# A float32 decoder trunk with routed experts on one core: the order of ScalarE and VectorE instructions around the small expert groups

## The chip, the cores and the metric

The kernel runs on one NeuronCore of one Trainium2 chip. The metric is the device time of one execution in microseconds (us); lower is better. A core has a matrix engine (TensorE, PE in the profile, with its weight loads as PEld), VectorE (DVE), ScalarE (ACT), GpSimd (POOL) and SyncE (SP), which here issues nearly all DMA transfers. Each engine works through its own queue of instructions in the order in which the program holds them, and waits at an instruction until the semaphores that it needs are set.

## The reference, cut to what matters

Two layers; the first has a dense SwiGLU, the second a mixture of eight experts of which each token takes two. All is float32, with 256 tokens of width 1024 and 3584 hidden columns for each expert.

```python
def swiglu(h, wg, wu, wd):
    return (jax.nn.silu(h @ wg) * (h @ wu)) @ wd

def moe_swiglu(h, router, wg, wu, wd):
    ...
    out = jnp.zeros_like(h)
    for e in range(N_EXPERTS):
        out = out + gate_e[..., e:e + 1] * swiglu(h, wg[e], wu[e], wd[e])
    return out
```

## The kernel before

The expert layer takes most of the time: it begins at about 480 us of the profiled span and ends near 1386 us. The experts are sorted by how many tokens they have, and expert slots get 32, 64, 64 or 128 places (`SLOTS`). An expert with 128 places is worked on by class `Ffn` ("full"), one with 64 or 32 by class `Few` ("small"). The 3584 hidden columns are cut into 7 groups of 512. One step of the layer is one group of one expert, and `in_turn()` writes the order of the 56 steps out: 35 full ones and 21 small ones. Stretches in which full and small steps alternate stand at the beginning (small expert 1, 64 places), in the middle (small expert 3, 32 places, often two full steps to a small one) and at the end (small expert 7, 64 places); expert 5 has a stretch of full steps to itself.

A step has a gate product, an up product and, one step later, a transposition of their result (`turn`) and a down product (`down`). Each product reads 4 half tiles of weights of 128 x 1024 floats. For step `(e, g)` after `last` the loop does, in this order: `ffn[e].gate(g)`, `ffn[last[0]].turn(last[1])`, `ffn[e].up(g)`, `ffn[last[0]].down(last[1])`. So where a small step follows a full one, PE does the small gate product, transposes the full step's activations, does the small up product and then the down product of the full step.

A full step multiplies in three passes of a rounded format (`mm3`): every half tile is first split (`split`, lines 281 to 292) by ACT into a rounded part `whi` (L290) and by DVE into the rest `wlo` (L291). The pool `wsp` holds four of each, so a split can be made only when PE is done with the half tile four before. The activations are split likewise after the transposition, into `aTh` on ACT (L627) and `aTl` on DVE (L628). For each half of a down half tile `mm3` needs `whi` and `aTh` first, then `wlo`, then `aTl`. A small step needs no split: it multiplies the float32 tiles as they are (L675 for gate and up, L702 for down). Its activation is L681 on ACT, its product of gate and up L684 on DVE, and the copy of its transposed activations L692 on ACT. In a full step these are L607 and L616.

`Stream` brings the weights in the order in which they are used: its loads go into a ring of 14 tiles of 1 MB (`raw`, some of them in `hT`), and SP issues a load as soon as the ring's next tile is free. `more()` has up to `LEAD = 4` split half tiles traced ahead; tiles of small steps don't count. So during a full step's up product the program text has already split its four down half tiles, before the text of the small step's gate product comes to its end.

The text does not settle the order of an engine's queue. The framework's scheduler orders each queue by its own estimate of when an instruction can start, within the data dependences. `tc.issue_after(ins)` adds an edge: what is traced inside it stands behind `ins` in the queue of `ins`'s engine. The kernel has such an edge already for the transpositions, which stand behind the last matmul of the gate product of the next step (`ffn[e].mark`).

Of the kernel before, what the change touches and what calls it, by code (L numbers as in the profile page):

```python
# [10 lines left out]
F32 = mybir.dt.float32  # L11
# [3 lines left out]
AF = mybir.ActivationFunctionType  # L15
ALU = mybir.AluOpType
# [3 lines left out]
P = 128  # L20
# [76 lines left out]
def trunk(ctx: ExitStack, tc: tile.TileContext, a: dict, out: bass.AP):  # L97
    nc = tc.nc
    V, A, G, T = nc.vector, nc.scalar, nc.gpsimd, nc.tensor
# [160 lines left out]


    ring = [wraw] * RAW
    free, behind = [0], []
    turn = [0]

    def more_raw():
# [14 lines left out]
    def split(raw, shape, q):  # L281
        hi = wsp.tile([P, 1024], F32R, name="whi")
        lo = wsp.tile([P, 1024], F32R, name="wlo")
        half = raw[:, 1024 * q : 1024 * q + 1024]
        with ExitStack() as es:
            free[0] -= 1
            if free[0] < 0:
                for ins in behind:
                    es.enter_context(tc.issue_after(ins))
            A.activation(hi, half, AF.Copy)  # L290
            V.tensor_tensor(lo, half, hi.bitcast(F32), op=ALU.subtract)  # L291
        return [x.rearrange("p (a b) -> p a b", a=shape[0] // 2) for x in (hi, lo)]

    def by_quarter(src, shape):
# [8 lines left out]
    def weight(src, shape):  # L303
        raw = load(src, shape)
        return [split(raw, shape, q) for q in range(2)]
# [53 lines left out]
    with tc.tile_pool(name="rope0", bufs=1) as rp:  # L359
# [8 lines left out]
        for bits in (8, 9, 9):  # L368
            e = math.floor(math.log2(rest)) + 1 - bits
# [207 lines left out]
    class Ffn:  # L577
# [23 lines left out]
        def gate(self, g):  # L601
            def done(t, ps):
                s = self.s[g, t] = self.sp.tile([P, GW], F32, name="silu", bufs=2 * self.nt)
                if self.rs is None:
                    A.activation(s, ps, AF.Silu)
                else:
                    A.activation(s, ps, AF.Silu, scale=self.rs(t))  # L607
            self.product(self.wg, g, done)

        def up(self, g):  # L610
            def done(t, ps):
                s = self.s[g, t]
                if self.rs is None:
                    V.tensor_tensor(s, s, ps, op=ALU.mult)
                else:
                    V.scalar_tensor_tensor(s, ps, self.rs(t), s, op0=ALU.mult, op1=ALU.mult)  # L616
            self.product(self.wu, g, done)

        def turn(self, g):
            for t in range(self.nt):  # L620
                s = self.s.pop((g, t))
                pt = ptr.tile([P, 4, P], F32, name="ps_t")
                for c in range(4):
                    T.transpose(pt[:, c], s[:, c * P : (c + 1) * P], ident)  # L624
                hi = self.sp.tile([P, 4, P], F32R, name="aTh", bufs=self.nt)
                lo = self.sp.tile([P, 4, P], F32R, name="aTl", bufs=self.nt)
                A.activation(hi, pt, AF.Copy)  # L627
                V.tensor_tensor(lo, pt, hi.bitcast(F32), op=ALU.subtract)  # L628
                self.aT[g, t] = (hi, lo)

        def down(self, g, done):
# [23 lines left out]
    class Few:  # L655
# [22 lines left out]

        def gate(self, g):
            s = self.s[g] = self.sp.tile([P, self.nj * P], F32, name="silu", bufs=2)  # L680
            A.activation(s, self.product(), AF.Silu, scale=self.rs)  # L681

        def up(self, g):
            V.scalar_tensor_tensor(self.s[g], self.product(), self.rs, self.s[g], op0=ALU.mult, op1=ALU.mult)  # L684

        def turn(self, g):
            s = self.s.pop(g)
# [49 lines left out]
    def moe(i, norm, make_next):  # L737
# [74 lines left out]
        with ExitStack() as es:  # L812
            sp = es.enter_context(tc.tile_pool(name=f"mo{i}", bufs=1, reuse_waits="tile"))
            py = es.enter_context(tc.tile_pool(name=f"my{i}", bufs=1, space=PSUM, reuse_waits="tile"))
            xe, oh, ffn, place, of = {}, {}, {}, {}, {}
# [3 lines left out]
            def width(e):  # L819
                return SLOTS[RANKS[e]]  # L820

            def arrange():
# [27 lines left out]
                for src, dst in ((posm, posp), (gate, tokp[:, :, :NE])):  # L850
                    V.tensor_tensor(w, m[:, None].to_broadcast([P, NT, NE, NE]),
                                    src[:, :, None, :].to_broadcast([P, NT, NE, NE]), op=ALU.mult)
                    V.tensor_reduce(dst, w, axis=AX.X, op=ALU.add)
                V.tensor_copy(tokp[:, :, NE : NE + 1], tok[:, :, NE : NE + 1])

            def seat(e):

                oh[e] = [rt.tile([P, P], F32R, name=f"oh{t}") for t in range(NT)]
                for t in range(NT):
                    at = posp[:, t, e : e + 1]  # L860
                    w = width(e)
                    if w < P:
                        V.tensor_scalar(oh[e][t].rearrange("p (b n) -> p b n", n=w),
                                        row[:, None, :w].to_broadcast([P, P // w, w]), at, None, op0=ALU.is_equal)
                    else:
                        V.tensor_scalar(oh[e][t], row, at, None, op0=ALU.is_equal)
# [36 lines left out]
            def places(e):  # L903

                pb = ptr.tile([P, NT, P], F32, name="ps_t")
                for t in range(NT):
                    T.matmul(pb[:, t], (posp if e else posm)[:, t, e : e + 1].to_broadcast([P, P]), ident, start=True, stop=True)
                oT = sp.tile([P, NT, P], F32R, name="oT", bufs=2)
                c = C_COL + WIDTHS.index(width(e))
                V.tensor_scalar(oT, pb, cst[:, c : c + 1], None, op0=ALU.is_equal)  # L910
                place[e] = oT
# [3 lines left out]
            def weigh(e, n2):  # L915
                gs, ps = of[e][:, e : e + 1], ys[e][n2]
                yh = sp.tile([P, 512], F32R, name="yh")
                yl = sp.tile([P, 512], F32R, name="yl")
                A.activation(yh, ps, AF.Copy, scale=gs)
                V.scalar_tensor_tensor(yl, ps, gs, yh.bitcast(F32), op0=ALU.mult, op1=ALU.subtract)  # L920
                ys[e][n2] = (yh, yl)

            def scatter(e, n2, fed=None):
                (yh, yl), oT = ys[e][n2], place[e]
                cs = slice(512 * n2, 512 * n2 + 512)
                for t in range(NT):
                    pz = ptr.tile([P, 512], F32, name="ps_t")
                    T.matmul(pz, oT[:, t], yh, start=True, stop=False)
                    T.matmul(pz, oT[:, t], yl, start=False, stop=True)  # L929
                    V.tensor_tensor(xs[t][:, cs], xs[t][:, cs], pz, op=ALU.add)  # L930
                    if fed is not None:
                        fed.feed(t, n2)
# [33 lines left out]
            def enter(e):  # L966
                gather(e)
                slots(e)
# [3 lines left out]
            for n, (e, g) in enumerate(steps):  # L972
                over = [x for x in ends if ends[x] + 2 == n]
                if g == 0:
                    rs = of[e][:, NE : NE + 1]
                    if width(e) < P:
                        ffn[e] = Few(lambda k, x=xe[e]: x[:, k], rs, sp, py, stream, width(e), e % 2)
                    else:
                        ffn[e] = Ffn(None, None, None, lambda part, k, t, x=xe[e]: x[:, k, part], 1,
                                     lambda t, rs=rs: rs, sp, py, stream, e % 2)  # L980
                ffn[e].gate(g)
                for x in over:
                    scatter(x, 0)
                    weigh(x, 1)
                if last:
                    with tc.issue_after(ffn[e].mark):
                        ffn[last[0]].turn(last[1])
                ffn[e].up(g)
                if n == 0:
                    arrange()  # L990
                    seat(1)
                if n == 1 or g == NG - 1:
                    if coming < NE:
                        enter(coming)
                        coming += 1
                        if coming < NE:
                            seat(coming)
                    elif e % 2 == 0:
                        fin_g = hpool.tile([P, D], F32, name="mT0")
                        G.dma_start(fin_g, a["final_norm"].partition_broadcast(P))  # L1000
                for x in over:
                    scatter(x, 1)
                if last:
                    ffn[last[0]].down(last[1], lambda t, ps, e=last[0]: ys.update({e: list(ps)}))
                    if last[1] == NG - 1:
                        weigh(last[0], 0)
                if g == NG - 2:
                    places(e)
                last = (e, g)
# [4 lines left out]
            e = NE - 1  # L1014
# [180 lines left out]
```

## Time and profile before

| | |
|---|---|
| runs | 1395.58 us median of 3 (1394.84 to 1399.27) |
| profiled execution | 1398.9 us, of it 1397.0 us span of instructions |
| granted TensorE clock, mean | 0.988 |
| PE busy | 1351.0 us, 97% of the span |
| DVE, ACT busy | 925.4 us (66%), 783.8 us (56%) |
| HBM read | 426.80 MB |

The time is that of the whole execution; the span is what the engines' instructions cover in it. Busy shares are means over stretches with different limits, so each stretch has to be looked at by itself. A line "A <- B: t, n, m" of the waits says that A waited for B t us in all, n times, at most m us. In a timeline the text in brackets is the idle time of the engine before the instruction and what ended it. Matmuls overlap, and their ends are modelled, so the time from start to start is what counts.

### The profile page before, as it was taken

Reading aid. Unit: us, or ns where it says so; the run is one execution under the profiler, and the core shown is the slowest. Engines: PE = TensorE matmul, PEld = TensorE weight load, DVE = VectorE, ACT = ScalarE, POOL = GpSimd, SP = SyncE. Lnnn points to the kernel's source line nnn. Section 1 sums busy time; section 2 is a strip of 40 time slices with the busy share of each in tenths; the row PEclk is TensorE's granted clock in tenths of the full one; section 3 lists DMA queues with packets and bytes.
Section 4 is the critical chain, followed back from the end, with each engine's and each line's share of the span. In section 5 each row is a group of like instructions: output and inputs, shape, how many; then the busy total and the mean of one; then the engine's idle time right before and its main releaser. Section 6 shows DMA issues by size and latency. Waiting matters only on the chain. (4 is left out here: it accounts for less than half of the span.)

```text
span 1397.0 us, 20471 instructions
## 1 busy us (share of the span) xinstructions
PE 1351.0 (97%) x7737; PEld 1039.8 (74%) x7737; DVE 925.4 (66%) x1450; ACT 783.8 (56%) x1118; POOL 7.3 (1%) x17
## 2 busy tenths in 40 slices
PE   7999999999999999999999999999999999999995
PEld 6888888888798787777666777777777788766662
DVE  7887544444787876655545776785679888644553
ACT  6867444444677556544444665665567777444442
POOL 1000000000000000000000000000000000000000
PEclk9999999999999989999999999999999999999998
DMA  8334554555333788999999999999999998999970
GB/s 336 106 136 144 190 184 184 187 185 188 137 135 138 281 313 310 401 421 420 394 408 344 418 419 403 417 420 420 420 421 411 365 361 316 375 401 416 419 312 32
DMA packets 60680, 429.23 MB, mean 307 GB/s; under 512 B 7089, under 2 KB 7281, under 8 KB 8993
## 3 DMA queue, kind: packets, MB, share of 16 engines
q1 hardware_dynamic: 59920, 425.85, 77.0%
q0 software_dynamic: 656, 2.02, 0.4%
q8 instruction: 62, 1.02, 0.3%
q14 instruction: 42, 0.34, 0.1%
HBM read 426.80 MB, written 1.05 MB: 306 GB/s over the span
## 5 line engine op out<-in xcount | busy, mean ns | idle before, releaser
L291 DVE TENSOR_TENSOR wlo<-raw,whi 128x1024 fp32r<-128x1024 f32 x528 | 626.5, 1221 | 164.6 <-ACT whi L290 158.6
L290 ACT ACTIVATE whi<-raw 128x1024 fp32r<-128x1024 f32 x528 | 546.3, 1060 | 237.0 <-PE ps_y L339 117.4
L337 PE MATMUL ps_m<-whi,mT 128*128 128x512 f32 x624 | 251.7, 403 | 0.0
L338 PE MATMUL ps_m<-wlo,mT 128*128 128x512 f32 x624 | 250.1, 401 | 0.1
L339 PE MATMUL ps_m<-whi,mT 128*128 128x512 f32 x624 | 247.7, 397 | 0.0
L338 PE MATMUL ps_y<-wlo,aTh 128*128 128x512 f32 x392 | 158.2, 404 | 15.5 <-DVE wlo L291 15.5
L337 PE MATMUL ps_m<-whi,hT 128*128 128x512 f32 (+1 forms) x416 | 156.0, 376 | 0.5 <-ACT whi L290 0.4
L338 PE MATMUL ps_m<-wlo,hT 128*128 128x512 f32 (+1 forms) x416 | 155.3, 373 | 0.5 <-DVE wlo L291 0.5
L339 PE MATMUL ps_y<-whi,aTl 128*128 128x512 f32 x392 | 155.5, 397 | 0.0
L339 PE MATMUL ps_m<-whi,hT 128*128 128x512 f32 (+1 forms) x416 | 154.8, 372 | 0.0
L337 PE MATMUL ps_y<-whi,aTh 128*128 128x512 f32 x392 | 143.6, 405 | 0.8 <-ACT aTh L627 0.8
L338 PEld LDWEIGHTS ps_m<-wlo,mT 128*128 128x128 f32 x624 | 117.7, 189 | 32.3 <-DVE wlo L291 7.2
L337 PEld LDWEIGHTS ps_m<-whi,mT 128*128 128x128 f32 x624 | 117.7, 189 | 30.9 <-ACT whi L290 3.4
L339 PEld LDWEIGHTS ps_m<-whi,mT 128*128 128x128 f32 x624 | 117.8, 189 | 26.5
L675 PE MATMUL ps_m<-raw,mT 128*64 128x256 f32 (+1 forms) x1648 | 120.4, 327 | 0.0
L675 PEld LDWEIGHTS ps_m<-raw,mT 128*64 128x64 f32 (+1 forms) x1648 | 79.0, 123 | 39.4 <-issue 12.4
L628 DVE TENSOR_TENSOR aTl<-ps_t,aTh 128x512 fp32r<-128x512 f32 x49 | 33.1, 688 | 110.4 <-ACT aTh L627 110.4
L338 PEld LDWEIGHTS ps_y<-wlo,aTh 128*128 128x128 f32 x392 | 74.5, 190 | 39.3 <-DVE wlo L291 22.3
L681 ACT ACTIVATE silu<-ps_m,of 128x256 f32<-128x256 f32 (+1 forms) x21 | 9.2, 439 | 162.0 <-PE ps_m L675 162.0
L337 PEld LDWEIGHTS ps_y<-whi,aTh 128*128 128x128 f32 x392 | 73.3, 190 | 24.0 <-ACT whi L290 4.3
L337 PEld LDWEIGHTS ps_m<-whi,hT 128*128 128x128 f32 x416 | 78.5, 189 | 14.1 <-ACT whi L290 0.8
L338 PEld LDWEIGHTS ps_m<-wlo,hT 128*128 128x128 f32 x416 | 78.5, 189 | 13.8 <-DVE wlo L291 1.0
(215 smaller groups left out, 1281.7 us busy)
## 6 DMA issues: line engine op xcount, KB each, us to landing
raw<-in_moe_w_gate SPq DMA_DIRECT2D x104, 1024.0 KB, 9.1
raw<-in_moe_w_up SPq DMA_DIRECT2D x104, 1024.0 KB, 9.9
raw<-in_moe_w_down SPq DMA_DIRECT2D x103, 1024.0 KB, 9.7
raw<-in_w_in SPq DMA_DIRECT2D x18, 1024.0 KB, 6.9
raw<-in_dense_w_gate SPq DMA_DIRECT2D x14, 1024.0 KB, 4.8
raw<-in_dense_w_up SPq DMA_DIRECT2D x14, 1024.0 KB, 4.9
raw<-in_dense_w_down SPq DMA_DIRECT2D x14, 1024.0 KB, 4.8
raw<-in_w_out SPq DMA_DIRECT2D x8, 1024.0 KB, 4.8
```

What stands on the lines that cost most here:

```text
L290: A.activation(hi, half, AF.Copy)
L291: V.tensor_tensor(lo, half, hi.bitcast(F32), op=ALU.subtract)
L337: T.matmul(ps, xh, wh, start=start, stop=False)
L338: T.matmul(ps, xh, wl, start=False, stop=False)
L339: return T.matmul(ps, xl, wh, start=False, stop=stop).ins
L628: V.tensor_tensor(lo, pt, hi.bitcast(F32), op=ALU.subtract)
L675: self.mark = T.matmul(o, self.xT(k), wk[:, b], start=k == 0, stop=k == DK - 1).ins
L681: A.activation(s, self.product(), AF.Silu, scale=self.rs)
```

## The change

Four edges are added. `split` keeps its two instructions in `at_split`, and the copy of the transposed activations keeps its DVE instruction in `turned`. The small step's activation (gate) then stands on ACT behind the `whi` that was traced last; the `turn` of the step before it (transpositions, `aTh`, `aTl`) stands behind the last `whi` on ACT and the last `wlo` on DVE, where the present step is a small one; and the small step's product (up) stands on DVE behind the last `aTl`. No instruction is added or removed.

```diff
-    free, behind = [0], []
+    free, behind, at_split, turned = [0], [], [], []
...
-            A.activation(hi, half, AF.Copy)
-            V.tensor_tensor(lo, half, hi.bitcast(F32), op=ALU.subtract)
+            at_split[:] = [A.activation(hi, half, AF.Copy).ins, V.tensor_tensor(lo, half, hi.bitcast(F32), op=ALU.subtract).ins]
...
-                V.tensor_tensor(lo, pt, hi.bitcast(F32), op=ALU.subtract)
+                turned[:] = [V.tensor_tensor(lo, pt, hi.bitcast(F32), op=ALU.subtract).ins]
...
-            A.activation(s, self.product(), AF.Silu, scale=self.rs)
+            ps = self.product()
+            with tc.issue_after(at_split[0]):
+                A.activation(s, ps, AF.Silu, scale=self.rs)
...
-            V.scalar_tensor_tensor(self.s[g], self.product(), self.rs, self.s[g], op0=ALU.mult, op1=ALU.mult)
+            ps = self.product()
+            with ExitStack() as after:
+                if turned:
+                    after.enter_context(tc.issue_after(turned[0]))
+                V.scalar_tensor_tensor(self.s[g], ps, self.rs, self.s[g], op0=ALU.mult, op1=ALU.mult)
...
-                    with tc.issue_after(ffn[e].mark):
+                    with tc.issue_after(ffn[e].mark), ExitStack() as after:
+                        if width(e) < P:
+                            for ins in at_split:
+                                after.enter_context(tc.issue_after(ins))
                         ffn[last[0]].turn(last[1])
```

What the edges do to the queues shows in the program's rows (line, operation, output<-inputs, shape, how many in a row). First ACT in the last alternating stretch, one full and one small step, from the full step's gate activation on. Before:

```order
L607 ACTIVATE silu<-ps_m,of 128x512
L692 ACTIVATE aTh<-ps_t 128x256
L290 ACTIVATE whi<-raw 128x1024 x2
L681 ACTIVATE silu<-ps_m,of 128x256
L627 ACTIVATE aTh<-ps_t 128x512
L290 ACTIVATE whi<-raw 128x1024 x10
```

With the change (line numbers are those of the changed file: 606 for 607, 697 for 692, 682 for 681, 626 for 627):

```order
L606 ACTIVATE silu<-ps_m,of 128x512
L697 ACTIVATE aTh<-ps_t 128x256
L290 ACTIVATE whi<-raw 128x1024 x4
L682 ACTIVATE silu<-ps_m,of 128x256
L626 ACTIVATE aTh<-ps_t 128x512
L290 ACTIVATE whi<-raw 128x1024 x8
```

The two splits ahead of the small activation were the last two of the full step's up product; now the up product's four stand ahead of the full gate activation, the four of the down product ahead of the small activation and of `aTh`, and eight (next gate, next up) behind them.

DVE at the same place, from the full step's product of gate and up to the next one. Before:

```order
L616 SCALAR_TENSOR_TENSOR silu<-ps_m,of,silu 128x512
L628 TENSOR_TENSOR aTl<-ps_t,aTh 128x512
L684 SCALAR_TENSOR_TENSOR silu<-ps_m,of,silu 128x256
L291 TENSOR_TENSOR wlo<-raw,whi 128x1024 x12
```

With the change (615 for 616, 627 for 628, 689 for 684, 290 for 291):

```order
L615 SCALAR_TENSOR_TENSOR silu<-ps_m,of,silu 128x512
L290 TENSOR_TENSOR wlo<-raw,whi 128x1024 x4
L627 TENSOR_TENSOR aTl<-ps_t,aTh 128x512
L689 SCALAR_TENSOR_TENSOR silu<-ps_m,of,silu 128x256
L290 TENSOR_TENSOR wlo<-raw,whi 128x1024 x8
```

The four `wlo` of the down product stood behind `aTl` and behind the small step's product; now they stand ahead of both. In the first alternating stretch, before about 640 us, the queues of the two kernels are the same. SP's and POOL's queues are the same throughout.

## Rows read from the trace of the kernel before

**Rows 1.** The page, part 1: busy time of each engine.

```profile
PE 1351.0 (97%) x7737; PEld 1039.8 (74%) x7737; DVE 925.4 (66%) x1450; ACT 783.8 (56%) x1118; POOL 7.3 (1%) x17
```

**Rows 2.** Waits of PE, whole span: total us, times, longest.

```profile
PE ps_y L338 <- DVE wlo L291: 15.5, 15, 1.4
...
PE ps_t L899 <- DVE mT L893: 0.9, 1, 0.9
```

**Rows 3.** Waits of PE, 640 to 760 us.

```profile
PE ps_y L338 <- DVE wlo L291: 3.5, 3, 1.4
```

**Rows 4.** Waits of PE, 760 to 1000 us.

```profile
PE ps_y L338 <- DVE wlo L291: 5.7, 6, 1.0
```

**Rows 5.** Waits of PE, 1200 to 1360 us.

```profile
PE ps_y L338 <- DVE wlo L291: 6.3, 6, 1.1
```

**Rows 6.** Timeline of PE, one small step of 64 places: start, us, instruction.

```profile
1229.63 3.67 PE L675 MATMUL ps_m<-raw,mT 128*64 128x256 f32 x32
1233.23 0.74 PE L337 MATMUL ps_y<-whi,aTh 128*128 128x512 f32 x2
1235.02 0.50 PE L338 MATMUL ps_y<-wlo,aTh 128*128 128x512 f32 x1 [1.05 <-DVE wlo L291]
```

**Rows 7.** Timeline of ACT and DVE in the same step.

```profile
1230.29 3.89 ACT L290 ACTIVATE whi<-raw 128x1024 fp32r<-128x1024 f32 x4
...
1230.42 0.69 DVE L628 TENSOR_TENSOR aTl<-ps_t,aTh 128x512 fp32r<-128x512 f32 x1 [7.56 <-ACT aTh L627]
1233.35 0.48 DVE L684 SCALAR_TENSOR_TENSOR silu<-ps_m,of,silu 128x256 f32<-128x256 f32 x1 [2.23 <-PE ps_m L675]
1233.75 2.35 DVE L291 TENSOR_TENSOR wlo<-raw,whi 128x1024 fp32r<-128x1024 f32 x2
```

**Rows 8.** Timeline of DVE and PE, a small step of the first stretch.

```profile
600.15 0.75 DVE L616 SCALAR_TENSOR_TENSOR silu<-ps_m,of,silu 128x512 f32<-128x512 f32 x1 [3.57 <-PE ps_m L339]
600.82 4.62 DVE L291 TENSOR_TENSOR wlo<-raw,whi 128x1024 fp32r<-128x1024 f32 x4
608.39 0.69 DVE L628 TENSOR_TENSOR aTl<-ps_t,aTh 128x512 fp32r<-128x512 f32 x1 [2.95 <-ACT aTh L627]
...
611.20 0.50 PE L337 MATMUL ps_y<-whi,aTh 128*128 128x512 f32 x1
611.54 0.40 PE L338 MATMUL ps_y<-wlo,aTh 128*128 128x512 f32 x1
```

**Rows 9.** Stretches: length, busy PE, PEld, DVE, ACT, POOL; PE clock, DMA share, GB/s.

```profile
600.00:628.40 28.40, 28.40 (x159) 19.56 (x158) 16.27 (x15) 11.49 (x13) 0.00 (x0) 1.00 1.01 421
...
1252.10:1282.10 30.00, 28.93 (x160) 19.37 (x160) 15.82 (x15) 14.09 (x16) 0.00 (x0) 1.00 1.01 419
...
880.00:1040.00 160.00, 156.29 (x1193) 119.95 (x1192) 111.65 (x116) 94.04 (x109) 0.00 (x0) 0.99 1.01 419
```

**Rows 10.** Timeline of PE, up product of the full step after rows 6.

```profile
1248.88 0.40 PE L337 MATMUL ps_m<-whi,mT 128*128 128x512 f32 x1
1249.29 0.50 PE L338 MATMUL ps_m<-wlo,mT 128*128 128x512 f32 x1
```

**Rows 11.** Timeline of PE, one small step of 32 places.

```profile
967.56 1.93 PE L702 MATMUL ps_y<-raw,aTh 128*32 128x512 f32 x16
...
974.09 0.74 PE L337 MATMUL ps_y<-whi,aTh 128*128 128x512 f32 x2
975.76 0.50 PE L338 MATMUL ps_y<-wlo,aTh 128*128 128x512 f32 x1 [0.94 <-DVE wlo L291]
```

**Rows 12.** Loads of down tiles and their first use (ACT), two places; time to landing.

```profile
1201.58 2.06 SPq L278 DMA_DIRECT2D raw<-in_moe_w_down  x2
973.34 1.32 SPq L278 DMA_DIRECT2D raw<-in_moe_w_down  x2
...
raw<-in_moe_w_down SPq DMA_DIRECT2D x6, 1024.0 KB, 18.8
...
1001.59 2.00 ACT L290 ACTIVATE whi<-raw 128x1024 fp32r<-128x1024 f32 x2
```

## The prediction

> **What bounds the kernel now.** I began with the page's table of busy times: PE is busy for 1351.0 of 1397.0 us, DVE for 925.4, ACT for 783.8 [rows 1]. So PE sets the time, 46 us of it idle, and a change of order on ACT and DVE is worth what PE idles for it and no more. Next the waits of PE, to see which of them lie in the places where the queues change. One line fits: the first matmul of a full step's down product with `wlo` waits for the split on DVE, 15 times, 15.5 us in all, 1.4 at most [rows 2]. Cut by stretches it stands 3 times in 640 to 760 us, 6 times in 760 to 1000, 6 times in 1200 to 1360 [rows 3 to 5]: wherever a small step follows a full one, except at the beginning.
>
> The timelines say why. PE ends the small up product at about 1233.3, starts the down product on `whi` and `aTh` at once, does two matmuls, and waits 1.05 us for `wlo` [rows 6]. ACT had begun those `whi` at 1230.29. DVE did `aTl` at 1230.42, idled 2.23 us at the small step's product, which wants PE's up product, and only then, at 1233.75, began the splits [rows 7]. DVE is not short of time; one instruction that waits for PE stands ahead of four that don't, and PE then waits for those four.
>
> In the first alternating stretch the same work stands in the other order: DVE does four `wlo` at 600.82, right after the full step's product, then `aTl` at 608.39, and PE goes from `whi` at 611.20 to `wlo` at 611.54 without a wait [rows 8]. That is a row of the order which the change writes for all small steps, in the same kernel. One full and one small step take 28.40 us there and 30.00 us from 1252.1 to 1282.1, for the same instructions, at a granted clock of 1.00 in both (the upper level, 2.4 GHz) [rows 9].
>
> **The change part by part.** No work is added or removed, so its cost is only what it makes wait.
>
> *Turn behind the splits (DVE).* This takes `wlo` from behind the small product to ahead of `aTl`. For 64 places the pair of stretches above prices it with all that follows: 30.00 - 28.40 = 1.60 us a pair [rows 9]. Of it 1.05 is the wait itself [rows 6]; another part is that DVE, late by then, is late again for the next up product, where the step from `whi` to `wlo` is 0.41 us, 1248.88 to 1249.29 [rows 10], against 0.34 in the undisturbed place [rows 8]; the rest is the refilling of PE after a wait. In the last stretch there are 6 such steps: 6 x 1.6 = 9.6 us, between 6.3 (the waits alone [rows 5]) and 9.6. In 640 to 760 there are 3, also of 64 places: between 3.5 (the waits alone [rows 3]) and 3 x 1.6 = 4.8; I take 1.5 each, 4.5. In the stretch of 32 places there are 6 with 5.7 us of wait, 0.95 each [rows 4]. No row shows that case in the new order; below it is the wait alone, 0.95, above it the 1.6 of the larger step. I take 1.2, since the wait is a tenth shorter and PE's following product meets DVE less late: 7.2 us. Sum: 9.6 + 4.5 + 7.2 = 21.3 us, from 15.5 (all waits, nothing behind them) to 15 x 1.6 = 24.0.
>
> *Does the turn come late instead?* `aTl` now stands behind four `wlo`, 4.62 us of DVE [rows 8]. In the 64-place step it waited there 2.95 us for `aTh` all the same, and was done 2.1 us ahead of PE's first down matmul [rows 8], so the splits cost nothing. With 32 places the small products are half as long. From PE's end of the full up product to its first down matmul there are 974.09 - 967.56 = 6.5 us [rows 11]. The full step's product (0.75) and four `wlo` (4.62) take 5.4 us of them, `aTl` 0.7 more: 6.1, and PE wants `aTl` only after `wlo`. So about half a microsecond to one is left. If that cover is gone, each microsecond by which `aTl` is late costs PE one, at 6 places.
>
> *Activation behind the last `whi` (ACT), `aTh` behind it.* The four `whi` take 3.89 us [rows 7], and each can be made once PE leaves the half tile four before, so three are done while the up product still runs and the last ends about 1 us behind it (an estimate: one split is 3.89 / 4 = 0.97). The small gate product takes some 3.7 us at 64 places, going by the up product of the same shape [rows 6], and half that at 32 (the small down product before it takes 1.93 there [rows 11]), so the activation would have to wait for the gate product anyway. Nothing is lost, as long as the weights of the down product have landed.
>
> *Product behind `aTl` (DVE).* It waits for PE's up product in any case, 2.23 us [rows 7], and its result is wanted a step later. Nothing.
>
> *What else is moved.* In 32-place stretches gathers and scatters of other experts share ACT and DVE. A copy that falls behind four splits could make PE wait; the nearest row is one wait of 0.9 us for a copy of DVE [rows 2]. I take 1.5 us off for this, between 0 and 4.
>
> The sum is about -20 us. The profiled execution took 1398.9 us (span 1397.0), 3.3 more than the median of 1395.58 that I predict against: 1395.6 - 20 = 1376.
>
> **The weight stream.** A faster PE must be fed. A pair of 64-place steps reads 12 tiles of 1 MB, 12.58 million bytes; at the 419 to 421 GB/s with a DMA share of 1.01 in all these stretches [rows 9] that is 29.9 to 30.0 us. So transfers can't keep a period of 28.4; the first stretch ran on a stock of tiles, and the later ones must too. In the last one a down tile issued at 1201.58 is split at 1230.29 [rows 7, 12]; taking off some 6 us for landing, about 22 us of lead. The earlier split eats up to 10 of it (PE needs the splits 11 us behind the full up product [rows 8], ACT began them 2.9 us before that need [rows 6, 7], and the first of them may now come ahead of the up product's end), five pairs eat 5 x 1.6 = 8, so some 4 are left: enough. Between 880 and 1040 it is tighter: a tile issued at 973.34 lands after 18.8 us, at 992.1, and is split at 1001.59, 9.5 later [rows 12]; the new order takes it up to 6.5 us sooner, and three or four steps of 1.2 us in that stretch come on top. That just about holds. Expert 5's full steps refill the stock behind it.
>
> The Trainium skill (*DMA: Bandwidth & Descriptors*, "Where 436 GB/s comes from") says that HBM reads bind at about 358 GB/s a core and that the fabric's ceiling is 435. By 358 a pair would take an estimated 35 us, which this case's 419 to 421 GB/s and 30.00 us contradict; by 435 it would be an estimated 28.9, so most of the gain would stay without any stock.
>
> **The rivals.**
>
> *The stream sets the pace.* If the stock is smaller than I count, a pair still takes 30 us in the last stretch, and the gain there and in 880 to 1040 (some 4 of 6 steps, 1.2 each) is gone. For it: DMA share 1.01 and 30.0 us by bytes. Against it: 22 us of lead. Time: 1395.6 - (21.3 - 9.6 - 4.8) = about 1389, or 1384 where half of the last stretch's gain is kept.
>
> *The wait only moves.* `aTl`, now behind four splits, is late in its turn, or PE meets the same `wlo` one step later. For it: the margin of half a microsecond at 32 places. Against it: the first stretch has that order and no such wait. At the 32-place steps alone this gives 1383 (7.2 less, and the 1.5 off); at all of them about 1395.
>
> *Slower: the activation and `aTh` stand behind a split that waits for its tile.* On ACT one late down tile now holds the small activation, then `aTh`, then PE's down product. Before, `aTh` stood ahead of these splits. The cover is about 1.5 us at 32 places (`aTh` done some 5 of the 6.5 us behind the up product [rows 11]). Each microsecond of lateness beyond that costs PE one a step. It decides when 12 steps (both saturated stretches) lose on average more than 20 / 12 = 1.7 us, so with down tiles over 3 us later than ACT reaches them; at 4 us it is 12 x 2.5 = 30 us against 20 gained: 1405. The leads of 22 and 9.5 us speak against it.
>
> The Trainium skill (*TensorE: Matmul & The Clock Gate*, "Architectural detail") says that ACT and DVE are strict FIFO while PE may pull weight loads ahead. By that rule nothing behind a late `whi` can pass it, which is what this rival needs; the trace agrees, with DVE idle for 2.23 us at a product while ready splits stood behind it [rows 7].
>
> *The clock.* The stretch from 880 to 1040 has a mean of 0.99 [rows 9]: 1.6 us lost to the lower level, 1.2 GHz, in a short drop. A drop more or less, since idle time moves, is some 1.6 us either way. It widens the range only.
>
> **How the numbers follow.** Forecast, with each case's own scatter: 0.72, 1369 to 1382 (24 us and a drop less at one end, 15.5 with 1.5 off at the other). The stream sets the pace: 0.14, 1383 to 1390. The wait moves: 0.07, 1383 to 1396. Slower: 0.07. About 0.3%, 4.2 us, is what a measurement of this kernel can tell from no change. Faster by more: 0.72 + 0.14 and half of a wait that moves only at some places, less a little for surprises: 0.87. Within: 0.06. Slower: 0.07. The range goes from 1369 to 1387, the middle of the stream's case; what lies beyond is some 0.15.
>
> **What would show it.** In the profile of the changed kernel the wait of `ps_y` L338 for `wlo` is gone or down to one or two; from 1190 on DVE has four `wlo` between the product of the full step and `aTl`, and a pair takes about 28.4 us. DVE's share stays, PE's rises to 98%. The stream rival shows as a pair of 30 us with a wait of ACT for `raw`; the slower one as PE waiting for `aTh` while ACT waits at a `whi`; the moved wait as PE waiting for `aTl`. I am wrong if the 1.6 us between the two stretches come from something other than this order, above all from the larger stock of tiles at 600 us.

## The result, and the profile after

The changed kernel takes 1417.14 us (median of 3, 1414.61 to 1417.71) against 1395.58: 1.0143 times as long, 95% interval 1.0109 to 1.0176. It is slower, by 21.6 us, where 20 us less were forecast. The profiled execution has a span of 1415.8 us, 18.8 more than before.

The page's busy times, as in [rows 1]:

```profile
PE 1364.7 (96%) x7737; PEld 1054.9 (75%) x7737; DVE 932.9 (66%) x1450; ACT 792.3 (56%) x1118; POOL 7.3 (1%) x17
```

The same instructions keep PE busy for 13.7 us more, which no added wait explains: the matmuls themselves take longer. The mean granted clock says so too, 0.973 against 0.988. In time lost to the lower level, that is (1 - 0.973) x 1415.8 = 38.2 us against (1 - 0.988) x 1397.0 = 16.8, or some 21 us more.

The waits of PE, as in [rows 2] (total us, times, longest; line 337 and 338 are the former 338 and 339, line 336 the former 337):

```profile
PE ps_y L338 <- DVE aTl L627: 15.8, 5, 3.3
...
PE ps_y L336 <- ACT aTh L626: 2.3, 2, 1.5
...
PE ps_y L337 <- DVE wlo L290: 1.7, 2, 1.3
```

The 15 waits for `wlo` are down to two, as forecast. In their place stand five for `aTl` that are three times as long. Two pairs of a small and a full step in the last stretch, the down product in which the first of the five waits lies, and the 11.5 us behind it (columns as in [rows 9]):

```profile
1271.50:1300.00 28.50, 28.50 (x161) 19.61 (x160) 16.27 (x15) 14.54 (x16) 0.00 (x0) 1.00 1.01 421
1300.00:1328.40 28.40, 28.40 (x159) 19.58 (x158) 16.27 (x15) 14.54 (x16) 0.00 (x0) 1.00 1.01 421
704.90:716.80 11.90, 8.72 (x26) 6.59 (x25) 6.83 (x8) 3.17 (x3) 0.00 (x0) 0.71 1.01 421
716.80:728.30 11.50, 11.50 (x51) 9.01 (x49) 7.25 (x6) 9.23 (x10) 0.00 (x0) 1.00 0.96 355
```

The first two rows are the forecast gain: 28.4 us a pair instead of 30.00, without any idle time of PE. The third is a loss that the forecast lacked: one down product of 24 matmuls, which takes some 5.9 us where nothing waits, took 11.9 us, at a mean clock of 0.71. The timeline of that place (ACT, then DVE, then PE; start, us, instruction, in brackets the idle time before it) shows how:

```profile
689.34 3.89 ACT L290 ACTIVATE whi<-raw 128x1024 fp32r<-128x1024 f32 x4
700.71 0.60 ACT L626 ACTIVATE aTh<-ps_t 128x512 fp32r<-128x512 f32 x1 [0.16 <-PE ps_t L623]
...
703.16 0.48 DVE L915 TENSOR_SCALAR oT<-ps_t,cst 128x256 fp32r<-128x256 f32 x1 [9.12 <-PE ps_t L912]
703.57 4.62 DVE L290 TENSOR_TENSOR wlo<-raw,whi 128x1024 fp32r<-128x1024 f32 x4
708.10 0.68 DVE L627 TENSOR_TENSOR aTl<-ps_t,aTh 128x512 fp32r<-128x512 f32 x1
...
705.27 0.39 PE L337 MATMUL ps_y<-wlo,aTh 128*128 128x512 f32 x1
708.84 0.80 PE L338 MATMUL ps_y<-whi,aTl 128*128 128x512 f32 x1 [3.17 <-DVE aTl L627]
709.43 0.63 PE L336 MATMUL ps_y<-whi,aTh 128*128 128x512 f32 x1
709.86 0.63 PE L337 MATMUL ps_y<-wlo,aTh 128*128 128x512 f32 x1
```

ACT has all four `whi` at 693 and `aTh` at 701. DVE could begin `wlo` at once, but its queue holds `oT` first, a copy that `places()` makes for putting the small expert's results back. `oT` waits for a matmul that PE does in the middle of the small up product, so DVE idles for 9.12 us with four ready splits behind it. Then come the four splits, 4.62 us, and only then `aTl`. PE waits 3.17 us, and behind the wait its matmuls follow each other every 0.43 us (709.43, 709.86) instead of every 0.23: the clock is at its lower level, 1.2 GHz.

Before the change the same copy stood there, but with `aTl` right behind it and the splits last. DVE in the kernel before:

```profile
701.83 0.48 DVE L910 TENSOR_SCALAR oT<-ps_t,cst 128x256 fp32r<-128x256 f32 x1 [7.32 <-PE ps_t L907]
702.23 0.68 DVE L628 TENSOR_TENSOR aTl<-ps_t,aTh 128x512 fp32r<-128x512 f32 x1
705.45 0.48 DVE L684 SCALAR_TENSOR_TENSOR silu<-ps_m,of,silu 128x256 f32<-128x256 f32 x1 [2.53 <-PE ps_m L675]
705.85 6.89 DVE L291 TENSOR_TENSOR wlo<-raw,whi 128x1024 fp32r<-128x1024 f32 x6
```

That cost PE one wait of 1.05 us for the first `wlo` and left the clock at 1.00. Such work for the seats of an expert (copies of places, of gathered tokens, additions of results) stands at six of the small steps: numbers 13, 15, 17, 31, 33 and 54 of the order of steps, counted from 0. Four of the five waits for `aTl` are at 13, 15, 17 and 31, the fifth, at 1374 us, at 54; at 33 PE waits 1.5 us for `aTh`. The other five have the same picture on DVE: the splits stand behind a copy of gathered tokens for which DVE idles 14.34 us at 15 and 5.03 at 33, behind a copy of places with 3.82 us at 31 and 9.32 at 54, and behind additions of results with several shorter pauses at 17.

### The profile page after: what moved, and what is told of

Same layout as the page of the kernel before. It is cut to its first block, busy times and chain, and to the rows that moved or that the text cites. A ratio compares the mean times of both kernels' runs of the same rounds, so it can differ in the third digit from the quotient of the medians.

```text
span 1415.8 us, 20535 instructions
## 1 busy us (share of the span) xinstructions
PE 1364.7 (96%) x7737; PEld 1054.9 (75%) x7737; DVE 932.9 (66%) x1450; ACT 792.3 (56%) x1118; POOL 7.3 (1%) x17
## 3 DMA queue, kind: packets, MB, share of 16 engines
HBM read 426.80 MB, written 1.05 MB: 302 GB/s over the span
## 4 chain that ended last, share of the span: by engine, by line
PE 93%; DVE 3%; DMA 2%; ACT 1%; issue 0%; SPq 0%; ACTq 0%; DVEq 0%
PE ps_m L337 16%; PE ps_m L336 16%; PE ps_m L338 16%; PE ps_m L674 8%; PE ps_y L338 7%; PE ps_y L336 7%; PE ps_y L337 7%; PE ps_y L707 4%; DVE wlo L290 2%; PE ps_t L623 2%; PE ps_s L459 1%; DMA raw<-in_moe_w_up 1%; PE ps_t L893 1%; PE ps_t L883 1%; PE ps_pt L483 1%; PE ps_o L488 1%
## 5 line engine op out<-in xcount | busy, mean ns | idle before, releaser
L290 DVE TENSOR_TENSOR wlo<-raw,whi 128x1024 fp32r<-128x1024 f32 x528 | 634.0, 1222 | 201.8 <-ACT whi L290 192.7
L290 ACT ACTIVATE whi<-raw 128x1024 fp32r<-128x1024 f32 x528 | 554.9, 1061 | 340.9 <-PE ps_y L338 194.8
L338 PE MATMUL ps_y<-whi,aTl 128*128 128x512 f32 x392 | 162.9, 417 | 15.8 <-DVE aTl L627 15.8
L337 PE MATMUL ps_y<-wlo,aTh 128*128 128x512 f32 x392 | 163.1, 416 | 1.7 <-DVE wlo L290 1.7
L336 PE MATMUL ps_y<-whi,aTh 128*128 128x512 f32 x392 | 161.2, 420 | 2.3 <-ACT aTh L626 2.3
L338 PEld LDWEIGHTS ps_y<-whi,aTl 128*128 128x128 f32 x392 | 78.3, 200 | 36.9 <-DVE aTl L627 18.0
L336 PEld LDWEIGHTS ps_y<-whi,aTh 128*128 128x128 f32 x392 | 78.8, 201 | 26.9 <-issue 5.6
L337 PEld LDWEIGHTS ps_y<-wlo,aTh 128*128 128x128 f32 x392 | 78.6, 201 | 20.6 <-DVE wlo L290 2.4
L336 PEld LDWEIGHTS ps_m<-whi,hT 128*128 128x128 f32 x416 | 78.7, 189 | 14.5 <-ACT whi L290 1.3
L338 PEld LDWEIGHTS ps_m<-whi,hT 128*128 128x128 f32 x416 | 78.6, 189 | 13.4
```

The costliest lines, as they stand in the source:

```text
L290: at_split[:] = [A.activation(hi, half, AF.Copy).ins, V.tensor_tensor(lo, half, hi.bitcast(F32), op=ALU.subtract).ins]
L336: T.matmul(ps, xh, wh, start=start, stop=False)
L337: T.matmul(ps, xh, wl, start=False, stop=False)
L338: return T.matmul(ps, xl, wh, start=False, stop=stop).ins
```

## Experiments

Theory A says that the loss is made in these six steps alone, by what stands ahead of the splits on DVE and by the clock behind the long wait, while the order is a gain everywhere else. The rivals are that the new order costs as such (B: on ACT, by the weight stream, or by the clock without a wait behind it), and that the gain was never there (C).

**Without the edges in the six steps.** All three places at which an edge is made ask for a flag, which each step sets:

```diff
+                edges[0] = n not in (13, 15, 17, 31, 33, 54)
...
-                        if width(e) < P:
+                        if width(e) < P and edges[0]:
                             for ins in at_split:
```

> The four edges are left out in six small steps (13, 15, 17, 31, 33, 54 of the order of steps), those in which DVE works on an expert's seats, gathered tokens or results between the full step's product and the splits, and kept in the other ten. Theory A (the loss is made in these six steps: a copy that waits for PE stands ahead of four splits, aTl comes some 3 us late, and TensorE falls to 1.2 GHz behind the wait): ten steps gain 1.5 us each, the six are as before: 1395.6 - 15 = 1380, granted clock back at 0.985 or more, no wait of PE for aTl over 1.5 us. Theory B (the new order costs as such, on ACT or by the weight stream, and the clock falls wherever PE gets no short pauses): still slower than before, 1400 or more, falls of the clock elsewhere. Theory C (the gain was never there): 1395.

Measured: 1384.95 us, 0.9915 of the kernel before (0.989 to 0.9939), clock 0.988. The waits of PE, and one stretch with a fall of the clock:

```profile
PE ps_y L337 <- DVE wlo L290: 5.6, 6, 1.4
```

```profile
840.00:858.00 18.00, 17.09 (x79) 14.11 (x77) 11.96 (x15) 9.57 (x11) 0.00 (x0) 0.81 1.01 419
```

No wait for `aTl` is left. Of the six for `wlo` five are those that the kernel before has in these six steps, and the sixth is of 0.2 us. The ten other steps give 12 us instead of 15. A pair of the last stretch gains 1.6 to 1.8 us, but one down product beside the gathering for expert 4, at 846 us, fell to the lower clock and gave 3 back (last row; two falls of 3.4 us each that the kernel before has at 738 and 1004 us are missing here, so the mean clock is the same). A holds, B and C fall.

**With the edges in the six steps only.** The same flag, `n in` instead of `n not in`.

> The opposite: the four edges only in those six steps. Theory A: the ten others wait for wlo as before (ten waits, 1.4 us at most), the six wait some 3 us each for aTl or aTh and fall to 1.2 GHz: 1395.6 + 5 x 6 = 1425, between 1417 and 1435, above the changed kernel because the gain of the ten is missing. Theory B: between the two kernels or below, 1395 to 1408, since only six of the edges are there. Theory C: 1417.

Measured: 1418.88 us, 1.016 (1.0135 to 1.0184), clock 0.980.

```profile
PE ps_y L338 <- DVE aTl L627: 12.5, 5, 3.4
PE ps_y L337 <- DVE wlo L290: 11.8, 12, 1.3
```

Both kinds of wait stand side by side. Six edges alone make the kernel 22 us slower, which B did not allow; C's 1417 is near it, but C fell with the run before. The size is at the lower end of A's: the five waits for `aTl` are 12.5 us in all instead of 15.8, since two of them, at 707 and at 1376 us, are of 1.45 us only.

**The copies behind `aTl`.** Of the six steps four get the edges back, and what stood ahead of the splits gets an edge itself:

```diff
+                edges[0] = n not in (17, 33)
...
+                        with ExitStack() as after:
+                            if n == 15:
+                                after.enter_context(tc.issue_after(turned[0]))
+                            enter(coming)
...
+                    with ExitStack() as after:
+                        if width(e) < P:
+                            after.enter_context(tc.issue_after(turned[0]))
+                        places(e)
```

> The edges stand in all small steps but two (17, the results of the first small expert, and 33, the gathering for a full one); in the four others of the six, DVE's copies for the places and for the gathered tokens get an edge themselves, behind aTl. Theory A: 14 steps gain 1.5 us, nothing waits long: 1395.6 - 21 = 1375, between 1371 and 1381, clock 0.985 or more. If a copy that is now late holds a buffer that PE wants, one wait of 2 to 5 us for it appears and the time is 1378 to 1385. Theory B: 1400 or more.

Measured: 1379.07 us (median of 5, 1375.4 to 1380.08), 0.9862 (0.9838 to 0.9886), clock 0.988: faster than both kernels. The waits of PE for `wlo`, two pairs of the last stretch, the stretch of 32 places, and one stretch with a fall of the clock:

```profile
PE ps_y L337 <- DVE wlo L290: 1.1, 2, 0.9
```

```profile
1239.10:1267.50 28.40, 28.40 (x159) 19.59 (x158) 16.26 (x15) 14.54 (x16) 0.00 (x0) 1.00 1.01 421
1267.50:1296.00 28.50, 28.50 (x161) 19.62 (x160) 16.27 (x15) 14.54 (x16) 0.00 (x0) 1.00 1.01 421
880.00:1040.00 160.00, 158.93 (x1206) 124.27 (x1206) 118.37 (x122) 99.89 (x113) 0.00 (x0) 1.00 1.01 421
838.00:856.00 18.00, 17.10 (x129) 14.17 (x132) 12.01 (x15) 8.79 (x10) 0.00 (x0) 0.81 0.94 392
```

DVE at step 13, the place shown above:

```profile
694.34 4.62 DVE L290 TENSOR_TENSOR wlo<-raw,whi 128x1024 fp32r<-128x1024 f32 x4
701.71 0.69 DVE L627 TENSOR_TENSOR aTl<-ps_t,aTh 128x512 fp32r<-128x512 f32 x1 [2.75 <-ACT aTh L626]
705.43 0.48 DVE L691 SCALAR_TENSOR_TENSOR silu<-ps_m,of,silu 128x256 f32<-128x256 f32 x1 [3.03 <-PE ps_m L674]
705.83 0.48 DVE L917 TENSOR_SCALAR oT<-ps_t,cst 128x256 fp32r<-128x256 f32 x1
```

Now DVE waits where nothing is behind it that PE wants soon, and `oT`, 2.7 us later than it was, holds nobody up. The stretch from 880 to 1040 us has PE busy for 158.93 us instead of 156.29 in [rows 9]. What is left is the fall at 845 us, a mean of 0.81 over 18 us, 3.4 us of clock.

**Waits of graded length.** This asks what a wait costs beyond itself. In the kernel before, `aTl` is written several times over in four undisturbed steps, which holds up `wlo` behind it:

```diff
-                V.tensor_tensor(lo, pt, hi.bitcast(F32), op=ALU.subtract)
+                for _ in range(1 + again[0]):
+                    V.tensor_tensor(lo, pt, hi.bitcast(F32), op=ALU.subtract)
...
+                again[0] = {46: 4, 48: 5, 50: 6, 52: 7}.get(n, 0)
```

> The kernel before, with aTl written again 4, 5, 6 and 7 times in small steps 46, 48, 50 and 52 of the last stretch (the same values; each write holds DVE for 0.6 us, so the wait of PE for wlo grows from 1.05 us to about 1.3, 1.9, 2.5 and 3.1 us). Theory A, that the long wait itself makes the clock fall: behind the wait of 3.1 us the granted clock is at the lower level for some 7 us and the down product takes 3.4 us longer; behind 1.3 us it stays at 1.00; where in between it begins is what the run shows. Time 1395.6 + 4.5 of waits + 3.4 to 7 = 1403 to 1407. Theory B, that the clock follows the order and not the wait: 1.00 in all four places, 1400.

Measured: 1410.63 us (one run), 13.6 us more than the 1397.03 of the kernel before beside it. The four waits, from the timeline, and then 12 us around each (the number behind the engines' busy times is the clock):

```profile
1236.33 0.50 PE L338 MATMUL ps_y<-wlo,aTh 128*128 128x512 f32 x1 [1.63 <-DVE wlo L291]
1269.23 0.50 PE L338 MATMUL ps_y<-wlo,aTh 128*128 128x512 f32 x1 [2.35 <-DVE wlo L291]
1301.28 0.50 PE L338 MATMUL ps_y<-wlo,aTh 128*128 128x512 f32 x1 [3.07 <-DVE wlo L291]
1335.68 0.49 PE L338 MATMUL ps_y<-wlo,aTh 128*128 128x512 f32 x1 [3.67 <-DVE wlo L291]
```

```profile
1232.00:1244.00 12.00, 10.37 (x48) 7.47 (x45) 10.92 (x12) 6.76 (x8) 0.00 (x0) 0.86 1.01 424
1265.00:1277.00 12.00, 9.65 (x47) 7.15 (x44) 11.90 (x13) 7.28 (x8) 0.00 (x0) 1.00 1.00 420
1297.00:1309.00 12.00, 8.93 (x34) 6.52 (x31) 10.93 (x12) 5.33 (x6) 0.00 (x0) 0.86 1.01 424
1331.00:1343.00 12.00, 8.32 (x31) 6.15 (x28) 10.93 (x13) 4.74 (x6) 0.00 (x0) 0.86 0.98 375
```

Three of four waits are followed by a fall, each (1 - 0.86) x 12 = 1.7 us of clock; the falls are half as long as expected. The time lies above A's 1403 to 1407, with waits that came out longer than expected (1.63 to 3.67 us instead of 1.3 to 3.1). The shortest has one and the second does not, so it is not the length alone. The kernel before has the same four steps with waits of some 1.05 us and a clock of 1.00.

**The same, the other way round**, with 7, 6, 5 and 4 more writes.

> The graded waits the other way round: aTl is written again 7, 6, 5 and 4 times in small steps 46, 48, 50 and 52 of the kernel before. Before, waits of 1.63, 3.07 and 3.67 us were followed by a fall of 3.4 us and the one of 2.35 us was not. If the length of the wait decides, the falls are at 46 and 48 (3.7 and 3.1 us) and one of the two others may be without; if it is the place, step 48 is without a fall and the three others have one; if it is chance, some other pattern. Time 1403 to 1412.

Measured: 1409.81 us (one run), waits of 3.68, 3.08, 2.35 and 1.63 us in this order:

```profile
1232.00:1244.00 12.00, 8.32 (x33) 5.87 (x30) 10.55 (x14) 4.66 (x5) 0.00 (x0) 0.72 1.00 410
1268.00:1280.00 12.00, 8.92 (x42) 6.62 (x39) 11.86 (x14) 6.54 (x7) 0.00 (x0) 1.00 1.00 408
1300.00:1312.00 12.00, 9.65 (x38) 7.07 (x35) 10.76 (x13) 5.92 (x6) 0.00 (x0) 0.86 1.01 426
1332.00:1344.00 12.00, 10.37 (x54) 7.60 (x51) 11.90 (x13) 7.98 (x8) 0.00 (x0) 1.00 1.01 425
```

Step 48 is without a fall again, with 3.08 us now, step 46 has one of twice the length; 1.63 us had a fall before and has none here, 2.35 us the other way round. Neither length nor place decides alone. Which of the waits is followed by a fall stays open; that such waits are followed by one in five of eight places is what the two runs show.

**Work for PE in the pause.** The changed kernel, and in five of the six steps 13 or 14 more matmuls ahead of the down product, into a buffer that nobody reads:

```diff
+            FILL = {13: 14, 15: 14, 17: 14, 31: 13, 54: 14}
...
+                    d = pmm.tile([P, 512], F32, name="ps_m")
...
+                    for _ in range(FILL[n]):
+                        T.matmul(d, th[:, 0], wh[:, 0, :512], start=True, stop=True)
```

> The changed kernel, and in five of the six steps (13, 15, 17, 31, 54) PE does 13 or 14 more matmuls of 0.23 us, whose result is not used, between the small up product and the full down product, that is in the time in which it waits for aTl. DVE and ACT have the same work, aTl comes as late as before, so no time is won by itself. Theory A (the pause of PE makes the clock fall): no wait for aTl over 1 us, the falls of the clock in these five places vanish, 27 us at the lower level fewer, half of it is time: 1417 - 13 = 1404, between 1400 and 1408. Theory B (the clock falls for another reason, such as the order or the load): the matmuls change nothing or cost their time, 1416 to 1425, clock 0.973.

Measured: 1402.94 us (median of 10, 1398.34 to 1406.7), 1.0035 (1.0018 to 1.0052), clock 0.983 to 0.988; the profiled execution took 1398.43 us, at 0.988. More work on the busiest engine makes the changed kernel 14 us faster. PE at step 13, and the clock from there on:

```profile
700.67 3.53 PE L1017 MATMUL ps_m<-whi,aTh 128*128 128x512 f32 x14
704.04 0.40 PE L336 MATMUL ps_y<-whi,aTh 128*128 128x512 f32 x1
704.27 0.39 PE L337 MATMUL ps_y<-wlo,aTh 128*128 128x512 f32 x1
704.58 0.50 PE L338 MATMUL ps_y<-whi,aTl 128*128 128x512 f32 x1
```

```profile
703.90:716.00 12.10, 12.10 (x54) 9.51 (x53) 9.06 (x10) 7.81 (x8) 0.00 (x0) 1.00 1.01 419
```

At steps 13, 17, 31 and 54 DVE and ACT have the rows of the changed kernel. At 13 DVE idles for the same 9.12 us ahead of `oT` and starts `aTl` 4.94 us behind it, as without the matmuls; only the pause is filled, and the clock stays at 2.4 GHz. That the falls in these four places come from PE's pause is shown by this, and A's size is met. Step 15 shows less: two of its four splits also moved ahead of the copy, and a fall of 3.4 us, instead of 10.2, lies under the added matmuls. Step 33 was not filled and still has a fall, of 6.8 us.

**Which edge does it.** Two runs divide the four edges. First only the one that the prediction priced, `aTl` behind the last `wlo` on DVE:

```diff
-            with tc.issue_after(at_split[0]):
-                A.activation(s, ps, AF.Silu, scale=self.rs)
+            A.activation(s, ps, AF.Silu, scale=self.rs)
...
-                if turned:
-                    after.enter_context(tc.issue_after(turned[0]))
...
-                            for ins in at_split:
+                            for ins in at_split[1:]:
```

> Of the four edges of the change only one is kept, aTl behind the last wlo on DVE; ACT's two edges and the one of the small product are left out. Theory A (this edge does both, the gain of 1.5 us in ten steps and the late aTl in six): 1412 to 1420, five or six waits for aTl of 2.5 to 3.4 us. Theory B (the edges on ACT hold aTh or the activation): 1380 to 1400.

Measured: 1482.38 us, 1.0597 (1.0573 to 1.0621), clock 0.961. No theory had that. The waits of PE, and one step of the last stretch on DVE and PE:

```profile
PE ps_y L338 <- DVE aTl L627: 47.7, 15, 3.3
PE ps_y L337 <- DVE wlo L290: 13.9, 13, 1.1
```

```profile
1324.69 0.48 DVE L686 SCALAR_TENSOR_TENSOR silu<-ps_m,of,silu 128x256 f32<-128x256 f32 x1 [10.49 <-PE ps_m L674]
1325.09 4.62 DVE L290 TENSOR_TENSOR wlo<-raw,whi 128x1024 fp32r<-128x1024 f32 x4
1329.62 0.69 DVE L627 TENSOR_TENSOR aTl<-ps_t,aTh 128x512 fp32r<-128x512 f32 x1
...
1330.36 1.22 PE L338 MATMUL ps_y<-whi,aTl 128*128 128x512 f32 x2 [3.28 <-DVE aTl L627]
```

Without ACT's edges the splits stay behind the small product on DVE, and the one edge that is kept only draws `aTl` behind them as well. So 15 small steps wait as the six did (step 9 is one of them now, 11 and 33 are not), and lose (1482.4 - 1397.2) / 15 = 5.7 us each: (47.7 + 13.9 - 15.5) / 15 = 3.1 more of wait, the rest by the clock.

Then the other three edges without that one (`at_split[:1]`).

> The opposite: ACT's two edges and the one of the small product are kept, aTl's edge on DVE is left out. Theory A: wlo stands behind aTl and the small product again, 15 waits for it, within 0.3% of the kernel before, 1392 to 1399. Theory B: slower, 1405 or more.

Measured: 1417.33 us, 1.0135 (1.0113 to 1.0157).

```profile
PE ps_y L338 <- DVE aTl L627: 15.8, 5, 3.3
```

This is the changed kernel again, and not A's 1392 to 1399: without that edge the scheduler puts DVE's rows in the same order, and the queues of ACT, DVE and PE are the same row by row. The gain and the loss both come by the other three edges. That it is ACT's two, which let `whi` be made ahead of the small activation, is likely but not shown: no run leaves out the small product's edge by itself.

## Why the prediction was wrong

*What bounds the kernel* was right, and so was the price of the waits. In the third experiment, with four of the six steps put in order and two left as they were, 13 of the 15 waits are gone and a pair takes 28.4 us, as in the first stretch [rows 9]; it takes 1379.1 us, 18.0 less than the kernel before beside it (1397.0), at the same mean clock of 0.988, where 20 less were forecast for the change.

*Turn behind the splits (DVE)* had the right sum and the wrong edge. DVE's own edge alone costs 85 us, and without it nothing changes. The prediction read the new rows of DVE and took them for the work of the edge on DVE; they come without it.

*What else is moved* is the step that failed. It says: "A copy that falls behind four splits could make PE wait; the nearest row is one wait of 0.9 us for a copy of DVE", and takes 1.5 us off, between 0 and 4. It looked at copies that come behind the splits. What happened is the reverse: splits, and with them `aTl`, came behind copies. By the starts of the down products in both timelines the six steps lose 2.5 to 7 us each net, 27 in all, the ten others gain 15, and falls of the clock in two full steps in which tokens are gathered (865 and 1172 us) add 5. *Does the turn come late instead?* counted from a DVE that is free 0.75 us after the full step's product; that holds in [rows 8], and not where a copy stands between, as at 703.16 us. The cover of 2.1 us before PE's need is then short by 3.2.

*The clock* was held to be "some 1.6 us either way". It cost some 21 us more than before. The prediction had 15 waits of about 1 us in its rows and none of 3 us, so nothing in them priced a longer one; that it needed a price of its own was not seen. Together: the waits are 15.8 + 2.3 + 1.7 us against 15.5 + 0.8, so 3.5 more (the 0.8 is one wait for `aTh` before). The clock adds some 21, less 2.6: of its time at the lower level 5.2 us lie in waits of PE, where they lengthen nothing. The wait at 747 us is one of these, at 0.50 throughout:

```profile
747.06:750.27 3.21, 0.00 (x1) 0.00 (x0) 3.21 (x5) 0.00 (x0) 0.00 (x0) 0.50 0.62 214
```

Some 5 go off, since a pair without a wait keeps PE busy for 28.4 us instead of 28.93 [rows 9], ten times. By this estimate the terms come to about 17 of the 18.8 between the spans.

*The rivals.* "The wait only moves" named `aTl` behind four splits, saw a short margin at the 32-place steps only, and priced it at the gain that is lost, 1383 to about 1395, no more. "Slower" named ACT and late tiles: ACT waited for weights for 6.0 us in all from 640 us on, and PE for `aTh` only 2.3, so it was not that. The rule that nothing passes a waiting instruction, which it drew from the Trainium skill (*TensorE: Matmul & The Clock Gate*, "Architectural detail"), was at work, but on DVE: 9.12 us of idle time with ready splits behind `oT`. *The weight stream* held: DMA at 421 GB/s and 28.4 us a pair, fed from the stock of tiles. Between 880 and 1040 us it held by less than "just about": the prediction's own sum, 9.5 less 6.5 less three or four times 1.2, is below zero. In the third experiment ACT waits there for weights for 1.7 us in all, and none of PE's waits there is for a `whi` or `aTh`.

## What to carry to other kernels

Before drawing work forward behind an edge, list what else stands on that engine in each of the places that the edge touches, not in the typical one: here ten of sixteen places gained 1.5 us and six lost 2.5 to 7 us each. If PE's waits are not only counted but grouped by length, a change that trades 15 short ones for 5 long ones shows as the risk it is, since a long one may be paid twice. And an edge on one engine moves rows on others, so the run without an edge is what tells which one matters.

## What the runs showed of the hardware that was not expected

A wait of PE can cost more than its length. In the kernel before, none of its 15 waits for `wlo`, up to 1.4 us, has a fall of the clock behind it; in the run with DVE's edge alone each of the 15 waits for `aTl`, of 2.6 to 3.3 us, has one beside it, of 3.4 or 6.8 us and once of 10.2 at 1.2 GHz, and matmuls that follow each other every 0.23 us do so every 0.43 us then. The Trainium skill (*TensorE: Matmul & The Clock Gate*, "HAM oscillation — how this bites in real kernels") tells of work behind a wait that starts at the lower clock; the runs agree, and add that filling the wait with matmuls of no use is worth 14 us here. What decides whether a given wait is followed by a fall is open: waits of 1.63, 2.35 and 3.07 or 3.08 us were once with and once without one. The largest loss of the six, some 7 us at step 33, has a wait of only 1.53 us and a fall of 10.2. Nor has every fall a wait ahead of it: in the changed kernel the one at step 15 begins 1.5 us before the long wait, and at 1172 us the clock falls for 6.8 us without any wait of PE between 1150 and 1180. It does not look like chance from one execution to the next, though: the changed kernel and the run without DVE's edge on `aTl`, whose queues are the same, have in the one profile of each the same eight falls between 600 and 1380 us, in the same places and of the same lengths.
